# Even mixer of a hybrid trunk: S5 inputs projected first, S5 passes moved ahead, gate products put inside the heads, tables loaded from GpSimd's queue

## The chip, the cores and the metric

The kernel runs on one core of a Trainium2 chip. A core has five engines with a queue of instructions each: TensorE (PE, matmuls), VectorE (DVE), ScalarE (ACT), GpSimd (POOL) and SyncE (SP, which here only issues DMAs). Each engine works its queue in order; a semaphore makes it wait for another engine or for a DMA. The metric is the device time of one execution in microseconds (us), the median of several.

## The reference, cut to what matters

A trunk of two layers, each a half feed-forward step, a mixer and another half step, on 256 latent and 256 context tokens of width 1024. Layer 0 has the even mixer, which the change is about: attention over a latent (low rank) projection beside an S5 state-space stream.

```python
def even_mixer(h_ctx, h_lat, ...):
    cq, ckv, kr, s = split(h @ w_in, [384, 640, 672])       # widths 384, 256, 32, 512
    k_lat, v_lat = mla_keys_values(ckv, kr, kv_norm, w_ukv, cos, sin)
    q_lat = mla_queries(cq, q_norm, w_uq, cos, sin)          # rmsnorm, 8 heads of 64 + 32 rope
    o_lat = latent_attention(q_lat, k_lat, v_lat, k_ctx, v_ctx)
    s_lat_out, _ = s5_stream(s, ...)
    return concatenate([o_lat, s_lat_out]) @ w_out

def s5_stream(u, ...):                                       # 32 groups of 16 channels, 64 states
    for dr in range(2):                                      # forward and backward in time
        h = linear_scan(a, einsum('gpc,bngc->bngp', b_bar, u))
        y += real(einsum('gcp,bngp->bngc', c_mat, h))
    y = gelu(y + d_skip * u)
    return y * sigmoid(y @ w_glu + b_glu)
```

## The kernel before, in words

All matmuls of the dense layers (`mm3`, lines 154 to 163) split both operands into a high and a low part in fp32r and do three matmuls for each 128 rows of the inner dimension. `wload` brings a weight on SP's queue, ACT casts its high part (line 150), DVE subtracts to get the low part (line 151). There are four buffers for raw and four for split weights, six PSUM tiles `mm` and two `ps`. The Tile framework orders each engine's instructions when the program is built; the order of the code gives it what depends on what and what comes first among equals.

While the first feed-forward step runs, a background job (`s5_chunk`, eight chunks) makes the S5 tables in DRAM: `d_mb`, `d_g`, `d_v` and `d_e`. The even mixer then runs in this order. `norm_proj` normalises the stream and does the first three projections in one loop, the blocks of `EVEN` (7 and 8: the keys' latent; 4: the first third of the queries'). The other blocks follow: 5, 6 (queries' latent), 9 (the rope part of the keys), 0 to 3 (S5 input `u`, which goes to DRAM as `d_u` and comes back rearranged as `ut`). `low_norm` normalises the two latents: squares on ACT, a column of sums on PE (line 255), the inverse root in small DVE steps (lines 266 to 275), a spread over 128 rows on PE (line 284), a product on DVE (line 780) and a split (lines 166, 167). Then come the values, and four pairs of heads, each with keys and queries (rope: lines 887 to 892), and eight heads with scores (907 to 925), transposed probabilities (940 to 947) and values (959).

The S5 stream is cut into eight passes of four groups. A pass has two halves. `s5_states` loads `d_mb` and `d_e`, does 8 matmuls of 64 columns and a chain on DVE (lines 994 to 1009, with a scan at 1003) whose end is the tile `hh`. `s5_out` loads `d_g` and `d_v` (eight DMAs, line 1021), does 12 matmuls (1025 to 1027) and stores `d_y`. Pass 0 stands beside the queries of pair 1, passes 1 and 2 beside those of pairs 2 and 3, the others beside the scores of the heads, one by one; the last `s5_out` comes after the last score. Behind the heads `s5_act` loads `d_u` and `d_y` on SP's queue (36 DMAs), applies the skip and GELU (1045) and splits; `s5_glu` does four gate products of 12 matmuls, a sigmoid (1063) and a product (1064). Then comes the output projection. Tiles of the passes and of `s5_act` are slots of one pool `x` with ten buffers, which also holds the normalised input of the projections and `ut`.

Of the kernel before, what the change touches and what calls it, by code (L numbers as in the profile page):

```python
# [18 lines left out]
P = 128  # L19
# [8 lines left out]
H = 8  # L28
# [10 lines left out]
EVEN, ODD = (7, 8, 4), (12, 13, 14)  # L39
# [26 lines left out]
class Builder:  # L66
# [581 lines left out]
    def s5_chunk(self, q):  # L648
# [73 lines left out]
        nc.sync.dma_start(self.d_v[q], vt)  # L722
        yield
# [18 lines left out]
    def s5_prepare(self):  # L742
        dt = lambda nm, shape: [self.dram.tile(shape, F32, tag=f"{nm}{q}", name=f"{nm}{q}") for q in range(NPASS)]
        self.d_mb = dt("d_mb", [P, 8, P])
        self.d_g = dt("d_g", [P, 8, P])
        self.d_v = dt("d_v", [P, 240])
        self.d_e = dt("d_e", [P, 2, 8, 64])
        yield from self.s5_small()
        for q in range(NPASS):
            yield from self.s5_chunk(q)  # L750


    def even_mixer(self):
# [39 lines left out]
        ut = [self.slot("x", [P, 16, NCH]) for _ in range(2)]  # L793
        for i in range(4):
            u = self.slot("q", [P, L, NCH])
            nc.scalar.copy(u, self.proj("ev_in", i, xs, 0, T2).rearrange("p (c s) -> p s c", s=L))
            nc.scalar.dma_start(d_u[i * P : (i + 1) * P], u)
            if i == 0:
                st["ckv"] = low_norm(ckv, self.inv_kv, 3)
            elif i == 1:  # L800
                st["cq"] = low_norm(cq, self.inv_q, 0)
# [25 lines left out]
        def keys(p):  # L827
# [17 lines left out]
        vt = values_in()  # L845
        st["wk"] = self.wload(t["wuk"], D)
        qs, ks = [], []
        passes = iter(range(NPASS + 1))
# [3 lines left out]
        def s5_begin():  # L852
            i = next(passes, None)
            state.append(None if i is None or i == NPASS else self.s5_states(i, ut))
            return i

        def s5_end(i):
            if i:
                self.s5_out(i - 1, ut, d_y, state[i])

        for p in range(4):
            ks.append(keys(p))
            i = s5_begin() if p else None
            qs.append(queries(p))
            s5_end(i)
        os = []
        pend = None
        for h in range(H + 1):
            i = s5_begin()
            pr = self.scores(qs[h // 2][:, h % 2, :], ks[h // 2][:, h % 2, :]) if h < H else None  # L870
            s5_end(i)
            if h == H:
                fin = self.s5_act(d_u, d_y)
            if pend is not None:
                pts = self.probs_t(pend)
                if h % 2 == 1:
                    first = pts
                else:
                    os.append(self.values(h - 2, vt, (first, pts)))
            pend = pr  # L880
        os += self.s5_glu(*fin)
# [89 lines left out]
    def s5_states(self, q, ut):  # L971

        nc = self.nc
        mb = self.slot("x", [P, 8, P])
        nc.sync.dma_start(mb, self.d_mb[q])
        et = self.slot("x", [P, 2, 512])
        nc.sync.dma_start(et, self.d_e[q].rearrange("p e g c -> p e (g c)"))
# [11 lines left out]
        ta, tb = self.slot("x", [P, 2, 512]), self.slot("x", [P, 2, 512])  # L989
# [11 lines left out]
        nc.gpsimd.memset(rz[:, :, 0:1], 0.0)  # L1001
# [6 lines left out]
        nc.gpsimd.memset(hv[:, :, 0:1], 0.0)  # L1008
# [3 lines left out]
    def s5_out(self, q, ut, d_y, hv):  # L1012
        nc = self.nc
        u = ut[q // 4][:, (q % 4) * 4 : (q % 4) * 4 + 4, :]
# [566 lines left out]
```

## Time and profile before

| what | value |
|---|---|
| median of 3 runs | 1766.3 us (1765.08 to 1766.74) |
| the profiled execution, its span | 1764.04 us, 1762.0 us |
| PE busy | 1702.8 us, 97% of the span |
| DVE busy | 1267.6 us, 72% |
| ACT busy | 693.7 us, 39% |
| POOL busy | 13.2 us, 1% |
| chain that ended last | PE 89%, DVE 6%, DMA 2% |

The busy times of an engine are those of its own instructions; they overlap with those of the others. Starts are counted from the start of the span. The even mixer's body, from the last matmul of `norm_proj` to the output projection, is the stretch from 442.5 to 619.2 us. Where a row gives "x4" it is a run of four instructions; the fp32 matmuls of the scores and passes leave two records each in the trace. The pitch of an instruction is the distance from its start to the next one's, which leaves the overlap out.

### The profile page before, as it was taken

The numbers are of one execution on the slowest core, as the hardware profiler recorded it, in microseconds if no ns is written. First come the engines' busy times: TensorE is split into PE (matmuls) and PEld (weight loads), VectorE is DVE, ScalarE is ACT, GpSimd is POOL, SyncE is SP. The second block draws the span as 40 slices with busy tenths as digits, with TensorE's granted clock in tenths as the row PEclk, the third lists the DMA queues.
The fourth block names the chain that finished last, engine by engine and source line by source line (L and its number), as shares of the span: only waits on it lengthen the run. The fifth ranks groups of instructions, "written<-read, shape, count | busy, mean of one in ns | idle before, by whom it ended". The sixth has DMA issues, their size and how long they took to land.

```text
span 1762.0 us, 24867 instructions
## 1 busy us (share of the span) xinstructions
PE 1702.8 (97%) x9380; PEld 1443.5 (82%) x9380; DVE 1267.6 (72%) x2545; ACT 693.7 (39%) x1101; POOL 13.2 (1%) x47
## 2 busy tenths in 40 slices
PE   5999999999989999999999999999999999699998
PEld 3788878889878788778888888888888888499998
DVE  7999999987488668776676686555543576976675
ACT  4433333443445654222222233222222357554443
POOL 0000000000000000000000000000000000000000
PEclk9999999999998999999999999999999999899999
DMA  9566767662465453564554443555533225155552
GB/s 330 172 221 213 228 212 229 215 189 95 126 188 166 132 188 107 171 216 147 164 190 157 159 141 124 181 185 155 169 120 96 96 96 187 67 171 189 183 183 90
DMA packets 107480, 292.65 MB, mean 166 GB/s; under 512 B 21152, under 2 KB 35360, under 8 KB 107104
## 3 DMA queue, kind: packets, MB, share of 16 engines
q1 hardware_dynamic: 101504, 286.86, 50.6%
q10 hardware_dynamic: 5216, 2.62, 0.8%
q0 software_dynamic: 640, 1.57, 0.3%
q8 instruction: 74, 1.21, 0.3%
q14 instruction: 46, 0.38, 0.1%
HBM read 272.20 MB, written 18.28 MB: 165 GB/s over the span
## 4 chain that ended last, share of the span: by engine, by line
PE 89%; DVE 6%; DMA 2%; issue 1%; SPq 1%; ACT 1%; DVEq 0%; ACTq 0%
PE mm L160 25%; PE mm L162 25%; PE mm L161 25%; PE mm L157 7%; DVE w L151 1%; DMA h<-in_modw_dram 1%; PE mm L1207 1%; SPq L1040 1%; DMA x<-d_g 1%; PE mm L907 1%; DVE x L322 0%; DVE nt L315 0%; PE mm L191 0%; PE ps L690 0%; PE ps L1118 0%
## 5 line engine op out<-in xcount | busy, mean ns | idle before, releaser
L150 ACT CAST w<-raw 128x1024 fp32r<-128x1024 f32 (+2 forms) x324 | 328.8, 1019 | 530.6 <-PE mm L162 262.2
L161 PE MATMUL mm<-x,w 128*128 128x512 f32 (+1 forms) x1424 | 519.8, 365 | 0.0
L162 PE MATMUL mm<-x,w 128*128 128x512 f32 (+1 forms) x1424 | 519.2, 365 | 0.0
L160 PE MATMUL mm<-x,w 128*128 128x512 f32 (+1 forms) x1424 | 514.6, 367 | 3.5 <-ACT x L320 2.2
L151 DVE TENSOR_TENSOR w<-raw,w 128x1024 fp32r<-128x1024 f32 (+2 forms) x324 | 383.8, 1186 | 150.5 <-ACT w L150 149.3
L160 PEld LDWEIGHTS mm<-x,w 128*128 128x128 f32 x1424 | 267.4, 189 | 49.5 <-ACT x L320 2.5
L161 PEld LDWEIGHTS mm<-x,w 128*128 128x128 f32 x1424 | 268.6, 189 | 43.8 <-issue 2.0
L162 PEld LDWEIGHTS mm<-x,w 128*128 128x128 f32 x1424 | 268.5, 189 | 43.9 <-issue 1.2
L227 DVE CUSTOM_DVE_ANT_0 junk<-m,sc 128x1024 f32<-128x1024 f32 x224 | 273.0, 1219 | 1.8 <-DMA m<-in_modw_dram 0.4
L160 PE MATMUL mm<-h,w 128*128 128x512 f32 x456 | 178.3, 394 | 0.0
L162 PE MATMUL mm<-h,w 128*128 128x512 f32 x456 | 176.9, 390 | 0.0
L161 PE MATMUL mm<-h,w 128*128 128x512 f32 x456 | 176.7, 390 | 0.0
L435 DVE SCALAR_TENSOR_TENSOR res<-mm,mraw,res 128x256 f32<-128x256 f32 x192 | 86.0, 479 | 96.5 <-PE mm L162 87.2
L471 DVE TENSOR_TENSOR h<-h,mm 128x512 f32<-128x512 f32 x66 | 45.3, 686 | 108.1 <-PE mm L162 95.8
L470 ACT ACTIVATE h<-mm 128x512 f32<-128x512 f32 x66 | 39.5, 598 | 196.0 <-PE mm L162 185.2
L160 PEld LDWEIGHTS mm<-h,w 128*128 128x128 f32 x456 | 85.6, 188 | 18.9 <-issue 1.1
L162 PEld LDWEIGHTS mm<-h,w 128*128 128x128 f32 x456 | 85.6, 188 | 18.5 <-issue 0.6
L161 PEld LDWEIGHTS mm<-h,w 128*128 128x128 f32 x456 | 85.6, 188 | 18.4 <-issue 1.0
L160 PE MATMUL mm<-hy,w 128*128 128x258 f32 x352 | 99.2, 284 | 0.7 <-DVE g L499 0.7
L162 PE MATMUL mm<-hy,w 128*128 128x258 f32 x352 | 99.6, 283 | 0.0
L161 PE MATMUL mm<-hy,w 128*128 128x258 f32 x352 | 99.6, 283 | 0.0
L157 PE MATMUL mm<-x,w 128*128 128x256 f32 x384 | 66.3, 290 | 6.7 <-DVE x L322 6.2
(371 smaller groups left out, 2002.1 us busy)
## 6 DMA issues: line engine op xcount, KB each, us to landing
raw<-in_wgu_dram SPq DMA_DIRECT2D x176, 512.0 KB, 3.9
m<-in_modw_dram SPq DMA_DIRECT2D x130, 512.0 KB, 4.3
raw<-in_wd_dram SPq DMA_DIRECT2D x64, 512.0 KB, 3.6
raw<-in_wd_dram SPq DMA_DIRECT2D x32, 384.0 KB, 3.3
raw<-in_od_in_dram SPq DMA_DIRECT2D x20, 512.0 KB, 3.5
h<-in_modw_dram SPq DMA_DIRECT2D x12, 512.0 KB, 10.0
raw<-in_ev_in_dram SPq DMA_DIRECT2D x10, 512.0 KB, 3.5
d_mb<-mbt SPq DMA_DIRECT2D x16, 256.0 KB, 3.4
```

The costliest lines, as they stand in the source:

```text
L150: nc.scalar.copy(hi[:, :n], raw[:, :n])
L151: nc.vector.tensor_sub(lo[:, :n], raw[:, :n], hi[:, :n])
L157: mm = lambda *a, **k: self.keep(self.nc.tensor.matmul(*a, **k))
L160: mm(ps, lhsT=wh, rhs=xh, start=first and i == 0, stop=False)
L161: mm(ps, lhsT=wh, rhs=xl, start=False, stop=False)
L162: r = mm(ps, lhsT=wl, rhs=xh, start=False, stop=last and i == n - 1)
L227: nc.vector.tensor_tensor_reduce(self.junk, w, self.sc[:, v, :], 1.0, 0.0, ALU.mult, ALU.add, raw[:, dt, v : v + 1])
L435: self.nc.vector.scalar_tensor_tensor(r, ps[:, c0:c1], gate[:, i, VEC[h] : VEC[h] + 1], r, op0=ALU.mult, op1=ALU.add)
L470: nc.scalar.activation(s[:, 0, lo:hi], pg[:, lo:hi], AF.Silu)
L471: nc.vector.tensor_mul(s[:, 1, lo:hi], s[:, 0, lo:hi], pu[:, lo:hi])
L907: nc.tensor.matmul(ps, lhsT=q[0:96, c : c + P], rhs=k[0:96, :nk], start=True, stop=True)
L1040: nc.sync.dma_start(uy[g * 16 : (g + 1) * 16, 1, :].rearrange("p (s n) -> p s n", s=L), d_y[i * 8 + g].rearrange("s c n -> c s n"))
```

## The change

Seven things change, all in the even mixer but for one.

1. `EVEN` is (0, 1, 2): the S5 inputs are projected first, then block 3, and their way through DRAM to `ut` starts there. Blocks 7, 8, 4, 5, 6, 9 follow.
2. The passes start earlier: pass 0 beside block 4, pass 1 beside block 6, pass 2 beside the values, pass 3 beside pair 0, pass 4 beside pair 2, passes 5, 6, 7 beside the scores of heads 1, 2, 4. The last `s5_out` stands beside the score of head 5.
3. `s5_act` is called at head 5, and the first gate products inside heads 7 and 8; the order in which the output projection takes its operands is changed to fit.
4. `d_mb`, `d_e`, `d_g` and the last table are loaded on GpSimd's queue, not SP's.
5. The eight DMAs from `d_v` become one from `d_z`, a rearranged copy that `s5_chunk` makes with four GpSimd DMAs in each chunk.
6. The stores of `d_y` go from GpSimd's queue to ACT's; eight copies of `kr` into the keys are DVE copies of 32x512 and no longer GpSimd DMAs; 16 small memsets go from GpSimd to DVE.
7. Tables and work tiles of passes 0 and 1 are slots of the pool `q`.

```diff
-EVEN, ODD = (7, 8, 4), (12, 13, 14)
+EVEN, ODD = (0, 1, 2), (12, 13, 14)
...
         nc.sync.dma_start(self.d_v[q], vt)
+
+        dv = self.d_v[q]
+        for g in range(4):
+            nc.gpsimd.dma_start(
+                self.d_z[q][:, g, :].rearrange("(r c) m -> r c m", r=L),
+                bass.AP(dv.tensor, dv.offset + g * 32 * 240, [[16, L], [240, 16], [1, P]]),
+            )
...
-        ckv = low(pss[:2])
-        cq = low(pss[2:] + [self.proj("ev_in", i, xs, 0, T2) for i in (5, 6)])
-        st["kr"] = self.slot("kr", [P, T2])
-        self.rope(st["kr"], self.proj("ev_in", 9, xs, 0, T2), ropet)
...
-                nc.gpsimd.dma_start(k[64:96, h, :], st["kr"][64:96])
+                nc.vector.tensor_copy(k[64:96, h, :], st["kr"][64:96])
...
+        def with_pass(work):
+            i = len(state) - 1
+            state.append(self.s5_states(i, ut) if i < NPASS else None)
+            r = work()
             if i:
                 self.s5_out(i - 1, ut, d_y, state[i])
+            return r
...
+        ckv = low([project(7), project(8)])
+        cq = [with_pass(lambda: project(4)), project(5)]
+        st["ckv"] = low_norm(ckv, self.inv_kv, 3)
+        cq = low(cq + [with_pass(lambda: project(6))])
+        st["kr"] = self.slot("kr", [P, T2])
+        self.rope(st["kr"], project(9), ropet)
+        st["cq"] = low_norm(cq, self.inv_q, 0)
+        vt = with_pass(values_in)
+        st["wk"] = self.wload(t["wuk"], D)
+        with_pass(lambda: pair(0))
+        pair(1)
+        with_pass(lambda: pair(2))
+        score = lambda h: self.scores(qs[h // 2][:, h % 2, :], ks[h // 2][:, h % 2, :])
+        pend = score(0)
+        pair(3)
+        os, glu = [], None
+        for h in range(1, H + 1):
+            pr = None
+            if h < H:
+                pr = with_pass(lambda: score(h)) if h in (1, 2, 4, 5) else score(h)
+            if h == 5:
+                glu = self.s5_glu(*self.s5_act(d_u, d_y))
+            pts = self.probs_t(pend)
...
+            if h > 6:
+                os.append(next(glu))
             pend = pr
-        os += self.s5_glu(*fin)
+        os = os[:3] + [os[4]] + [os[3]] + os[5:] + list(glu)
...
-        mb = self.slot("x", [P, 8, P])
-        nc.sync.dma_start(mb, self.d_mb[q])
-        et = self.slot("x", [P, 2, 512])
-        nc.sync.dma_start(et, self.d_e[q].rearrange("p e g c -> p e (g c)"))
+        tag = "q" if q < 2 else "x"
+        mb = self.slot(tag, [P, 8, P])
+        nc.gpsimd.dma_start(mb, self.d_mb[q])
+        et = self.slot(tag, [P, 2, 512])
+        nc.gpsimd.dma_start(et, self.d_e[q].rearrange("p e g c -> p e (g c)"))
...
-        gm = self.slot("x", [P, 8, P])
-        nc.sync.dma_start(gm, self.d_g[q])
-        tz = self.slot("x", [P, 4, P])
-        dv = self.d_v[q].rearrange("(g c) m -> c g m", g=4)[0:16]
-        for r in range(L):
-            nc.sync.dma_start(tz[r * 16 : (r + 1) * 16], dv[:, :, r * 16 : r * 16 + P])
+        gm = self.slot(tag, [P, 8, P])
+        nc.gpsimd.dma_start(gm, self.d_g[q])
+        tz = self.slot(tag, [P, 4, P])
+        nc.gpsimd.dma_start(tz, self.d_z[q])
...
-        nc.gpsimd.dma_start(d_y[q * 4 : (q + 1) * 4].rearrange("g s c n -> (s c) g n"), ys)
+        nc.scalar.dma_start(d_y[q * 4 : (q + 1) * 4].rearrange("g s c n -> (s c) g n"), ys)
```

The built program of the changed kernel shows where things stand. In what follows `mm` and `ps` are PSUM tiles, `c` the split latents, `p` the latents and the probabilities, `x` and `hh` the tiles of passes. First PE around the norm of the queries' latent. Before, 46 rows (of the built order) lie between the column sums (line 255) and the spread of the inverse root (line 284); this is the start of that stretch:

```order
L284 MATMUL ps_4267<-ident,rs_y_4274 128x128 x4
L255 MATMUL ps_4357<-inv_q,p_4348 128x1 x4
L162 MATMUL mm_4422<-x_3880,w_4419 128x512
L160 MATMUL mm_4422<-x_3881,w_4419 128x512
L161 MATMUL mm_4422<-x_3881,w_4419 128x512
```

and this its end, inside the values:

```order
L821 MATMUL mm_4513<-w_4492,c_4312 128x512
L822 MATMUL mm_4513<-w_4492,c_4312 128x512
L284 MATMUL ps_4356<-ident,rs_y_4363 128x128 x4
L823 MATMUL mm_4513<-w_4492,c_4312 128x512
L821 MATMUL mm_4521<-w_4492,c_4308 128x512
```

After, the spread stands two rows behind the sums:

```order
L1038 MATMUL ps_4488<-hh_4300,q_4484 128x64
L255 MATMUL ps_4555<-inv_q,p_4546 128x1 x4
L162 MATMUL mm_4727<-c_4423,w_4695 128x512
L284 MATMUL ps_4554<-ident,rs_y_4561 128x128
L998 MATMUL ps_4610<-x_4162,x_4606 128x64 x4
L1000 MATMUL ps_4610<-x_4162,x_4606 128x64 x4
L284 MATMUL ps_4554<-ident,rs_y_4561 128x128 x3
L1036 MATMUL ps_4677<-x_4162,q_4675 128x64
L1037 MATMUL ps_4677<-hh_4441,q_4673 128x64
L1038 MATMUL ps_4677<-hh_4441,q_4673 128x64
```

What was covered by block 1, part of block 2 and half of the values has one matmul of the keys between; the states of the third pass (lines 998, 1000) and the outputs of the second (1036 to 1038) come next.

Second, ACT in the last heads. `ACT_TABLE_LOAD` loads a set of activation functions. Before, the heads end (lines 916 to 947) and then the GELUs (1045) and the sigmoids (1063) follow:

```order
L947 COPY c_5557<-mm_5564 128x4x128
L941 COPY c_5632<-mm_5633 128x512
L1029 COPY ys_5439<-ps_5426 128x256
L947 COPY c_5639<-mm_5640 128x4x128
L1045 ACT_TABLE_LOAD
L1045 ACTIVATE x_5572<-x_5572 128x512
L947 COPY c_5639<-mm_5646 128x4x128
L166 CAST x_5584<-x_5572 128x512
L166 CAST q_5665<-mm_5652 128x512
L1045 ACTIVATE x_5587<-x_5587 128x512
L166 CAST x_5599<-x_5587 128x512
L1045 ACTIVATE x_5602<-x_5602 128x512
```

After, GELU (line 1056) stands between the exponentials (927) of the heads; this is head 6:

```order
L927 ACTIVATE p_5380,sm_st_5381<-mm_5382,sm_st_5381 128x256 x2
L1056 ACT_TABLE_LOAD
L1056 ACTIVATE x_5428<-x_5428 128x512
L166 CAST q_5377<-mm_5364 128x512
L166 CAST x_5440<-x_5428 128x512
L927 ACT_TABLE_LOAD
L927 ACTIVATE p_5392,sm_st_5393<-mm_5394,sm_st_5393 128x512
L927 ACTIVATE p_5392,sm_st_5393<-mm_5396,sm_st_5393 128x512
L1040 COPY ys_5423<-ps_5410 128x256
L952 COPY c_5488<-mm_5489 128x512
L936 ACTIVATE p_5392<-p_5392,sm_st_5393 128x512 x2
L958 COPY c_5495<-mm_5496 128x4x128
```

Each of the four GELUs of the changed kernel has a table load ahead of it and another behind it: eight loads from the first GELU to the first sigmoid, where there were two.

Third, the loads of the tables. Before, they share SP's queue with the raw weights:

```order
L144 DMA raw_5766<-in_ev_out_dram 128x1024
L1017 DMA x_4740<-d_g_138 128x1024
L1021 DMA x_4742<-d_v_146 16x4x128 x8
L975 DMA x_4779<-d_mb_132 128x1024
L977 DMA x_4781<-d_e_156 128x1024
L144 DMA raw_5802<-in_ev_out_dram 128x1024
L144 DMA raw_5840<-in_ev_out_dram 128x1024
L144 DMA raw_5878<-in_ev_out_dram 128x1024
L1017 DMA x_4845<-d_g_139 128x1024
L1021 DMA x_4847<-d_v_147 16x4x128 x8
```

After, they are alone on GpSimd's queue, in the order in which the passes need them, but for the first two passes' `d_g` and `d_z`, which stand behind the `d_mb` and `d_e` of the third:

```order
L987 DMA q_4285<-d_mb_130 128x1024
L989 DMA q_4287<-d_e_162 128x1024
L987 DMA q_4426<-d_mb_131 128x1024
L989 DMA q_4428<-d_e_163 128x1024
L987 DMA x_4606<-d_mb_132 128x1024
L989 DMA x_4608<-d_e_164 128x1024
L1030 DMA q_4484<-d_g_138 128x1024
L1032 DMA q_4486<-d_z_154 128x512
L1030 DMA q_4673<-d_g_139 128x1024
L1032 DMA q_4675<-d_z_155 128x512
L987 DMA x_4698<-d_mb_133 128x1024
L989 DMA x_4700<-d_e_165 128x1024
```

## Rows read from the trace of the kernel before

**Rows 1.** PE by stretch: us, busy (instructions), granted clock, DMA share, GB/s.

```profile
523.00:530.00 7.00, 0.00 (x0) 0.78 0.68 199
530.00:545.00 15.00, 14.75 (x60) 0.53 0.62 197
```

**Rows 2.** PE's waits, 440 to 660 us: us in total, times, longest.

```profile
PE ps L1025 <- DMA x<-d_v: 7.4, 1, 7.4
PE mm L959 <- ACT c L947: 1.2, 1, 1.2
PE mm L162 <- DVE w L151: 0.6, 1, 0.6
PE mm L160 <- ACT x L166: 0.4, 1, 0.4
...
PE mm L160 <- ACT w L150: 0.4, 1, 0.4
```

**Rows 3.** Waits of SP's DMA queue, 440 to 620 us.

```profile
SPq L1017 <- DVE x L995: 22.2, 4, 6.6
```

**Rows 4.** The chain that ended last, at the wait: start, us, what.

```profile
523.17 4.92 DMA x<-d_g
```

**Rows 5.** Timeline of PE: start, us, line, tiles, run length.

```profile
519.15 1.06 PE L988 MATMUL ps<-x,x 128*128 128x64 f32 x8
520.05 2.80 PE L907 MATMUL mm<-q,q 96*128 96x256 f32 x8
...
599.42 0.39 PE L1026 MATMUL ps<-hh,x 128*128 128x64 f32 x2
599.64 0.39 PE L1027 MATMUL ps<-hh,x 128*128 128x64 f32 x2
...
601.20 1.04 PE L946 MATMUL mm<-ident,p 128*128 128x128 f32 x8
...
615.91 1.08 PE L160 MATMUL mm<-x,w 128*128 128x512 f32 x4
616.83 0.39 PE L161 MATMUL mm<-x,w 128*128 128x512 f32 x1
```

**Rows 6.** Timeline of DVE where passes and queries overlap.

```profile
504.05 0.69 DVE L151 TENSOR_TENSOR w<-raw,w 128x512 fp32r<-128x512 f32 x1
504.66 1.22 DVE L1003 TENSOR_TENSOR_SCAN x<-x,x 128x512 f32<-128x512 f32 x1
505.91 0.75 DVE L892 TENSOR_TENSOR q<-q,nt 32x256 f32<-32x256 f32 x2
506.68 0.69 DVE L1004 TENSOR_TENSOR x<-x,x 128x512 f32<-128x512 f32 x1
507.38 0.69 DVE L994 TENSOR_TENSOR x<-x,x 64x512 f32<-64x512 f32 x1
508.08 0.69 DVE L995 TENSOR_TENSOR x<-x,x 64x512 f32<-64x512 f32 x1
...
523.21 1.29 DVE L913 TENSOR_REDUCE sm_st<-mm 128x1 f32<-128x512 f32 x2
```

**Rows 7.** Timeline of DVE in the inverse root of the queries' latent.

```profile
478.82 0.60 DVE L273 SCALAR_TENSOR_TENSOR rs_a<-rs_y,rs_v 128x1 f32<-128x1 f32 x4
479.34 0.36 DVE L275 SCALAR_TENSOR_TENSOR rs_y<-rs_a,rs_y 128x1 f32<-128x1 f32 x4
```

**Rows 8.** Timeline of ACT: exponential, scaling, PSUM copies, table load, GELU.

```profile
526.80 0.68 ACT L916 ACTIVATE p<-mm,sm_st 128x512 f32<-128x512 f32 x1
...
530.61 1.33 ACT L925 ACTIVATE p<-p,sm_st 128x512 f32<-128x512 f32 x2 [2.36 <-DVE sm_st L919]
...
589.26 1.09 ACT L947 COPY c<-mm 128x512 f32<-128x512 f32 x2
...
602.45 1.28 ACT L1045 ACT_TABLE_LOAD   x1
603.75 0.63 ACT L1045 ACTIVATE x<-x 128x512 f32<-128x512 f32 x1
```

**Rows 9.** DMA issues of GpSimd's queue: size, median us to landing.

```profile
d_y<-ys POOLq DMA_DIRECT2D x8, 128.0 KB, 2.9
```

More of the change, by code (lines that the diff above doesn't have):

```diff
@@ L746, in s5_prepare @@
         self.d_v = dt("d_v", [P, 240])
+        self.d_z = dt("d_z", [P, 4, P])
         self.d_e = dt("d_e", [P, 2, 8, 64])
@@ L793, in even_mixer @@
         ut = [self.slot("x", [P, 16, NCH]) for _ in range(2)]
+        project = lambda i: self.proj("ev_in", i, xs, 0, T2)
         for i in range(4):
             u = self.slot("q", [P, L, NCH])
-            nc.scalar.copy(u, self.proj("ev_in", i, xs, 0, T2).rearrange("p (c s) -> p s c", s=L))
+            nc.scalar.copy(u, (pss[i] if i < 3 else project(i)).rearrange("p (c s) -> p s c", s=L))
             nc.scalar.dma_start(d_u[i * P : (i + 1) * P], u)
[L798 to L801, printed above, removed]
             if i % 2:
@@ L843, in queries @@
             return q
-        vt = values_in()
-        st["wk"] = self.wload(t["wuk"], D)
         qs, ks = [], []
-        passes = iter(range(NPASS + 1))
         state = [None]
[L852 to L857, printed above, removed]
+        def with_pass(work):
+            i = len(state) - 1
+            state.append(self.s5_states(i, ut) if i < NPASS else None)
+            r = work()
@@ L858, in s5_end, with pair @@
             if i:
                 self.s5_out(i - 1, ut, d_y, state[i])
-        for p in range(4):
+            return r
+        def pair(p):
             ks.append(keys(p))
-            i = s5_begin() if p else None
             qs.append(queries(p))
[L865 to L879, printed above, removed]
+        ckv = low([project(7), project(8)])
@@ new lines, in even_mixer @@
+        pend = score(0)
[8 more added lines that the diff above has]
+            pts = self.probs_t(pend)
+            if h % 2 == 1:
+                first = pts
+            else:
+                os.append(self.values(h - 2, vt, (first, pts)))
+            if h > 6:
+                os.append(next(glu))
@@ L988, in s5_states @@
                 nc.tensor.matmul(o.rearrange("p (t c) -> p t c", t=2), lhsT=mb[:, k, :], rhs=rev(u[:, g, :]), start=True, stop=True)
-        ta, tb = self.slot("x", [P, 2, 512]), self.slot("x", [P, 2, 512])
+        ta, tb = self.slot(tag, [P, 2, 512]), self.slot(tag, [P, 2, 512])
         hh = self.slot("hh", [P, 512])
@@ L1000, in s5_states @@
         rz = tb[:, 1].rearrange("p (g c) -> p g c", g=8)
-        nc.gpsimd.memset(rz[:, :, 0:1], 0.0)
+        nc.vector.memset(rz[:, :, 0:1], 0.0)
         nc.scalar.copy(rz[:, :, 1:NCH], self.s5["rho"][:, q * 8 : q * 8 + 8].unsqueeze(2).to_broadcast([P, 8, NCH - 1]))
@@ L1007, in s5_states @@
         xv, yv = (a.rearrange("p (g c) -> p g c", g=8) for a in (x, y))
-        nc.gpsimd.memset(hv[:, :, 0:1], 0.0)
+        nc.vector.memset(hv[:, :, 0:1], 0.0)
         nc.vector.tensor_add(hv[:, :, 1:NCH], xv[:, :, 0 : NCH - 1], yv[:, :, 0 : NCH - 1])
@@ L1013, in s5_out @@
         nc = self.nc
+        tag = "q" if q < 2 else "x"
         u = ut[q // 4][:, (q % 4) * 4 : (q % 4) * 4 + 4, :]
         rev = lambda a: a.rearrange("p (t c) -> p t c", t=2)[:, :, ::-1]
-        gm = self.slot("x", [P, 8, P])
-        nc.sync.dma_start(gm, self.d_g[q])
-        tz = self.slot("x", [P, 4, P])
-        dv = self.d_v[q].rearrange("(g c) m -> c g m", g=4)[0:16]
-        for r in range(L):
-            nc.sync.dma_start(tz[r * 16 : (r + 1) * 16], dv[:, :, r * 16 : r * 16 + P])
+        gm = self.slot(tag, [P, 8, P])
+        nc.gpsimd.dma_start(gm, self.d_g[q])
+        tz = self.slot(tag, [P, 4, P])
+        nc.gpsimd.dma_start(tz, self.d_z[q])
         py = self.ps()
```

4 lines of the change are left out of this document (1 added, 3 removed).

## The prediction

> **What bounds the kernel now.** The page's first part says PE: 97% of the span, and the chain that ended last is PE for 89%. PE has little idle time to give back, so I looked for where it loses time in the mixer's body, 442.5 to 619.2 us. The waits of PE [rows 2] show one large one, 7.4 us, in front of the first S5 output of pass 1, for the tile loaded from `d_v`. [...] Half speed there costs 14.75 x 0.47 = 6.9 us. The chain [rows 4] and SP's waits [rows 3] show why the load was late: `d_g` of that pass was issued at 523.17 only, since its slot of the pool `x` was still being read by DVE (L995), and the `d_v` loads queue behind it. So behind the DMA stands DVE, which had been working without a gap. The other waits of the body are 1.2 + 0.6 + 0.4 + 0.4 = 2.6 us [rows 2], all near its end. Together PE loses 7.4 + 6.9 + 2.6 = 16.9 us in the body. That is all that a new order can win: the matmuls are the same.
>
> **The change part by part.** *What goes.* The wait of pass 1's output for `d_v` goes as it stood (its load has moved to another queue, its slot comes from the pool `q`), and the slow stretch behind it: 14.3 us. The 2.6 us near the end go with the gate products, which no longer stand alone there. I count -16.9 us.
>
> *The queries' norm.* Before, 45 matmuls and small ones lie between the sums (L255) and the spread (L284); after, one. DVE's root needs three rounds of 0.6 + 0.36 us less overlap [rows 7], 0.9 each, and three single steps of about 0.15, so 3 us, and PE has 0.23 us of work meanwhile. A wait of some 3 us; it is the first part of what comes next, and not added to it.
>
> *The stretch from that norm to the second head's transposes.* Here the new order puts passes 2 to 5, all query pairs and three heads' scores. PE's work in it: 91 matmuls of 512 columns at 0.23 (four from 615.91 to 616.83) [rows 5], 20.9; four outputs of 12 at 0.22 (the 0.22 from 599.42 to 599.64), 10.8; five states at 1.8 (their second half runs from 519.15 to 520.05), 9.0; three scores at 2.7, 8.1; twelve transposes at 0.13, 1.6; sums and spreads 0.9: 51.3 us [rows 5]. DVE's work in it: a pass is a scan at 1.25 and eight operations at 0.70, 6.85, and two memsets of under 0.1: four passes 28.0. Rope is 24 operations at 0.41, 9.9 [rows 6]. Five weight subtractions, 3.3. Three heads' maxima at 0.64 each with the small ones, 7.5 [rows 6]. The root 3.0 [rows 7], three products and three splits at 0.67, 4.0. Six of the eight new DVE copies, 32x512: no row shows one. [...] I take 0.45, nearest to the row of the same 32 partitions, 2.7. Sum 58.4, and 2.3 us in which DVE waits for the states of pass 2 behind the spread: 60.7. PE works in order, and its last rows here (transposed probabilities of head 1) need DVE's last ones, so PE loses 60.7 - 51.3 = 9.4 us. Bounds: with copies at 0.2 and half of DVE's wait covered, 7; with copies at 0.7 and each of the two score releases late by an exponential, 13. The moved `kr` copies and memsets cost nothing elsewhere: DVE has room in the projections and after head 2.
>
> *Between head 2 and head 6* PE and DVE are level and a few waits for scaled probabilities remain: 2 us, from 0 to 4, by the 1.2 us wait of L959 for ACT, which I expect about twice [rows 2].
>
> *GELU inside the heads.* From head 6's first exponentials to the last copy of transposed probabilities ACT has, one behind the other: six table loads at 1.30 (602.45 to 603.75), 7.8; six exponentials at 0.66 and six of half the width at 0.46 (an estimate from the former), 6.8; six scalings at 0.62, 3.7; twelve PSUM copies at 0.48, 5.8 [rows 8]; five casts and three GELUs at 0.6, 4.7; a store's issue and a copy, 0.8. Sum 29.6 us. PE's work in the same stretch is one S5 output, two scores, four heads' transposes, one values (3.2) and nine matmuls of the first gate product: 2.7 + 5.4 + 6.4 + 3.2 + 2.1 = 19.8 [rows 5]. PE waits for exponentials and copies in turn, so it loses 9.8 us. Before, these heads had no table load between them. Bounds: 0, if ACT enters the stretch ten microseconds ahead of PE; 13, if GELU also waits for its `d_y` there, since exponentials queue behind a GELU.
>
> [...]
>
> *Moved at no cost.* SP's queue loses 88 issues and gains none, so raw weights come earlier; the cover was there already. The 32 copies to `d_z` stand behind the `d_v` store on GpSimd's queue, with the next chunk's memset behind them; a chunk lasts over 40 us, GpSimd is 1% busy, and what it delays is background work under the dense first feed-forward: 0, up to 2 if a chunk slips into the mixer. The `u` stores and the first `ut` loads go to ACT 25 us earlier in the code, ahead of the casts of weights 4, 5 and 6; PE has two blocks (10 us) in front of the first states. 0, up to 3. The `d_y` stores add eight issues to ACT, of which one is in the sum above.
>
> *Sum.* -16.9 + 9.4 + 2.0 + 9.8 = +4.3 us. Against the profiled execution's own 1764.04 that is 1768.3; that execution lies 2.3 us under the median of the runs, so the forecast for the median is 1770.6, say **1771 us**. Its own range, from the bounds of the two large terms, is 1769.9 to 1778. New waits of 3 us could also bring the lower clock back; half of the old price, 3.5 us, is inside that range.
>
> **The rivals.** *A: faster.* The place is the last heads: ACT is not the bound there. If PE reaches head 6 late, as the DVE stretch makes it, ACT may have copied and scaled ahead by then; the table loads vanish under PE's work and the 9.8 go to 0, with the DVE stretch at its lower bound 7: -16.9 + 7 + 1.5 = -8.4, 1758 us. It decides from the point where ACT has a lead of over 6 us at head 6. For it: ACT is busy 39% of the span. Against: exponentials need scores that PE has just made, so ACT can't run far ahead.
>
> *B: no change that can be measured.* Half of the ACT term hidden: +4.3 - 4.9, 1765.7 us. A measurement of this kernel tells about 0.2%, 3.5 us, from no change.
>
> *C: the wait moves to GpSimd's queue.* The loads of `d_g` and `d_z` still need slots that DVE releases, and now stand in order behind the next passes' loads. If pass 2's `d_z` (slot released at the end of its chain on DVE) lands after PE is there, PE has another wait like the old one, 7.4 us at most, with or without the lower clock: 1771 + 7.4 = 1778 us and up to 1785. For it: the mean wait for such a slot was 5.5 us, 22.2 in 4 [rows 3]. Against: PE itself is late at that point, waiting for the same DVE, and GpSimd's DMAs land in 2.9 us in the median [rows 9]. [...]
>
> **How the numbers follow.** The forecast (slower, 1769.9 to 1778) has 0.42, A 0.20, B 0.26, C 0.12. Slower by over 0.2% (above 1769.8): 0.42 + 0.12 = 0.54. Within: 0.26. Faster: 0.20. The range that should hold 8 in 10 goes from 1757, which leaves out about half of A, to 1780, which leaves out half of C. Signs on both sides hold much of the chance; the likeliest case's own range stands above.
>
> **What would show it.** In the changed kernel's profile: no wait for `d_v` or `d_z` of over 2 us (else C); a wait of about 3 us of L284 for DVE; DVE busy without a gap from there until head 1's scores, and PE under 90% busy in that stretch; six table loads between the exponentials of the last heads, ACT without a gap there and PE waiting for ACT some 10 us in all; a clock of 1.00 in the projections. The body should be 4 us longer than 176.7. If PE is dense in the last heads, the ACT term is wrong; if DVE shows gaps in the stretch of passes 2 to 5, the DVE term is; a lower clock over a long stretch would put the time above the range.

## The result, and the profile after

The changed kernel takes 1775.1 us (median of 4 runs, 1774.8 to 1776.1), the kernel before, run beside it, 1765.7 (1764.1 to 1766.7). The ratio is 1.0057, with a 95% interval of 1.0044 to 1.007: slower by 9.4 us. The forecast was 1771 and slower, with a range from 1757 to 1780. So the sign and the range held, and the loss is about twice the forecast. The profiled execution has a span of 1772.9 us, 10.9 more than before, and all of it is in the mixer's body: the first matmul of the output projection on the attention's operands starts at 630.03 us, where it started at 619.16 before.

The page's first part (busy us, share of the span, instructions):

```profile
PE 1713.2 (97%) x9380; PEld 1449.5 (82%) x9380; DVE 1272.1 (72%) x2569; ACT 701.3 (40%) x1107; POOL 37.2 (2%) x79
```

PE does the same matmuls and is busy 10.4 us longer; the share of 97% hides it. Most of it is what matmuls at the lower clock look like on that line (the granted clock reads 0.50 or 1.00 in 1752 of 1760 windows of 1 us before and in 1748 after): by these windows, what the clock lacks (busy time times what it is short of 1.00) grew from 6.9 to 12.3 us in the body, and by 3.5 us behind it, where the span did not get longer. PE's waits between 436 and 660 us (us in total, times, longest):

```profile
PE mm L951 <- DVE p L934: 3.3, 1, 3.3
PE ps L284 <- DVE rs_y L275: 2.7, 1, 2.7
PE mm L957 <- ACT p L936: 2.4, 1, 2.4
PE mm L957 <- ACT p L927: 0.9, 1, 0.9
...
```

The old wait of 7.4 us for `d_v` [rows 2] has no heir: no row names a table. In its place stand a wait for the queries' norm, one for a probability that DVE scales, and a handful for ACT, 13.0 us in all where there were 10.4. The windows by stretch show where the body's time went (after the stretch and its length: busy us and instructions of PE, PEld, DVE, ACT, POOL; then the granted clock, DMA share, GB/s):

```profile
442.50:493.60 51.10, 51.10 (x266) 43.51 (x266) 33.85 (x70) 20.85 (x34) 5.27 (x10) 1.00 0.71 206
493.60:516.00 22.40, 18.83 (x78) 17.36 (x78) 16.00 (x49) 4.51 (x8) 2.11 (x4) 0.54 0.34 104
516.00:545.00 29.00, 29.00 (x163) 24.64 (x162) 26.59 (x55) 14.53 (x36) 4.24 (x8) 1.00 0.50 155
545.00:564.00 19.00, 15.75 (x91) 12.49 (x91) 17.97 (x41) 12.10 (x32) 2.13 (x4) 0.91 0.60 203
564.00:587.00 23.00, 23.00 (x156) 17.03 (x155) 18.16 (x40) 14.25 (x35) 2.21 (x4) 1.00 0.43 116
587.00:620.00 33.00, 26.86 (x141) 17.03 (x140) 13.26 (x33) 32.02 (x61) 0.00 (x0) 0.95 0.18 44
```

Read each as idle time plus busy time times what the clock lacks. From 493.6 to 516: 3.6 idle and 18.83 x 0.46 = 8.7, so 12.3 us. From 545 to 564: 3.25 + 1.4 = 4.7. From 587 to 620: 6.1 + 1.3 = 7.4. The other stretches are dense at full clock. Sum 24.4 us, against 17.3 before (10.4 of waits and 6.9 of half clock). The slow stretch is no longer 15 us at pass 1's output [rows 1] but 20 at the queries' norm. PE's timeline there (start, us, line, tiles, run length; in brackets the wait ahead of it):

```profile
493.60 0.48 PE L162 MATMUL mm<-c,w 128*128 128x512 f32 x1
496.81 0.76 PE L284 MATMUL ps<-ident,rs_y 128*128 128x128 f32 x2 [2.72 <-DVE rs_y L275]
497.36 1.81 PE L998 MATMUL ps<-x,x 128*128 128x64 f32 x8
498.96 1.91 PE L1000 MATMUL ps<-x,x 128*128 128x64 f32 x8
```

The four matmuls of the states' second half (two records each) take 1.91 us at line 1000; before they took 1.06 [rows 5]. DVE, which follows PE there, shows the other side (its marked idle times from 493 to 545 of 0.6 us or more):

```profile
493.78 0.16 DVE L266 TENSOR_SCALAR rs_v<-ps 128x4 f32<-128x4 f32 x1 [0.60 <-PE ps L255]
500.91 0.69 DVE L1009 TENSOR_TENSOR x<-ps,x 128x512 f32<-128x512 f32 x1 [4.04 <-PE ps L1000]
513.19 0.69 DVE L1009 TENSOR_TENSOR x<-ps,x 128x512 f32<-128x512 f32 x1 [1.84 <-PE ps L1000]
543.37 0.17 DVE L930 RECIPROCAL sm_st<-sm_st 128x2 f32<-128x2 f32 x1 [0.68 <-ACT p L927]
```

And ACT in the last heads, where it is busy 32.0 of 33 us: each GELU between two table loads, two of the eight shown.

```profile
587.90 1.28 ACT L1056 ACT_TABLE_LOAD   x1
589.19 0.63 ACT L1056 ACTIVATE x<-x 128x512 f32<-128x512 f32 x1
...
590.83 1.28 ACT L927 ACT_TABLE_LOAD   x1
592.13 0.69 ACT L927 ACTIVATE p<-mm,sm_st 128x512 f32<-128x512 f32 x1
```

### The profile page after: what moved, and what is told of

Same layout as the page of the kernel before. It is cut to its first block, busy times and chain, and to the rows that moved or that the text cites. A ratio compares the mean times of both kernels' runs of the same rounds, so it can differ in the third digit from the quotient of the medians.

```text
span 1772.9 us, 24792 instructions
## 1 busy us (share of the span) xinstructions
PE 1713.2 (97%) x9380; PEld 1449.5 (82%) x9380; DVE 1272.1 (72%) x2569; ACT 701.3 (40%) x1107; POOL 37.2 (2%) x79
## 4 chain that ended last, share of the span: by engine, by line
PE 88%; DVE 7%; ACT 2%; issue 1%; DMA 1%; SPq 0%; DVEq 0%; ACTq 0%
PE mm L160 25%; PE mm L161 25%; PE mm L162 25%; PE mm L157 7%; DVE w L151 1%; PE mm L1216 1%; DMA h<-in_modw_dram 1%; DMA raw<-in_wgu_dram 1%; DVE x L322 0%; ACT p L927 0%; PE mm L970 0%; PE ps L284 0%; DVE nt L315 0%; PE ps L690 0%; PE ps L1127 0%
```

## The experiments

Three things can have cost the time: the norm that lost its cover, DVE's full queue behind it, and the table loads in the heads. Two theories on the first two: either the lower clock is the price by itself, or DVE sets when the stretch ends, and PE's waits and clock only fill the time until then. "Body" is the start of that output projection's matmul; a ratio is that to the kernel before, run beside it.

**The norm covered.**

```diff
-            rb = self.rstd([acc], inv)
+            r = self.rstd_stats([acc], inv)      # sums and root here,
+            ...                                  # spread (rstd_rows), product and split in low_rest
-        st["cq"] = low_norm(cq, self.inv_q, 0)
+        r = low_norm(cq, self.inv_q, 0, split=True)
         vt = with_pass(values_in)
+        st["cq"] = low_rest(cq, r, 0)
```

> The changed kernel with the spread of the queries' inverse root put, in the code, behind the third pass and the values; in the built order 8 state matmuls of the third pass and 12 output matmuls of the second then stand between the column sums and the spread, 4 to 5 us of work at full clock. Theory 1 (the price of the clock): the wait of 2.7 us for DVE goes, PE keeps its upper clock from 495 to 516, where the changed kernel ran about 20 us at half, and the time falls by 9 to 12 us against the changed kernel, to 1763 to 1766. Theory 2 (DVE is the bound there, whatever PE's clock): DVE had gaps of only 0.6 + 4.0 + 1.8 = 6.5 us from 493 to 543, so no more than that can be won, 3 to 6.5 us, to 1769 to 1772, and PE waits more in front of head 1's transposes than the 3.3 us of now.

Measured: 1770.5 us, ratio 1.0028 [1.0017, 1.0039], 4.7 us less than the changed kernel; body 624.55, 5.5 less. PE's waits there, and two windows of PE (busy, instructions, clock, DMA share, GB/s):

```profile
PE mm L956 <- DVE p L939: 2.4, 1, 2.4
PE mm L160 <- ACT c L166: 2.4, 1, 2.4
...
PE ps L284 <- DVE rs_y L275: 0.6, 1, 0.6
```

```profile
490.00:500.00 10.00, 9.81 (x80) 1.00 0.40 121
500.00:510.00 10.00, 7.23 (x36) 0.85 0.51 164
```

The wait for the norm falls to 0.6 us, the 20 us at half clock shrink to about 4, and yet only 5.5 us are won: a new wait of 2.4 us for the split of the same latent appears at once. DVE is now busy from 495 to 559 us with marked gaps of 0.7 us in all. That is the size that the second theory gave; its other sign missed, as the wait in front of head 1's transposes did not grow from 3.3 us but fell to 2.4. The way from the column sums (line 255) to those transposes is 59.8 us, where it was 67.4. Of the nine executions, the one with the highest mean clock (0.991) took 1767.9 us and the one with the lowest (0.984) 1776.1; the profile is one of them, of 1769.3 us.

**The gate products behind the heads.**

```diff
-            if h == 5:
+            if h == H:
                 glu = self.s5_glu(*self.s5_act(d_u, d_y))
...
-            if h > 6:
-                os.append(next(glu))
-        os = os[:3] + [os[4]] + [os[3]] + os[5:] + list(glu)
+        os += list(glu)
...
-            nc.scalar.activation(y, y, AF.Gelu_apprx_tanh)
+            self.keep(nc.scalar.activation(y, y, AF.Gelu_apprx_tanh))   # behind ACT's earlier instructions
```

> The changed kernel with the skip and GELU called at the last step of the heads and all four gate products behind the heads, each GELU held behind the activations written ahead of it: two table loads from the heads' end to the first sigmoid in place of eight. Theory 1 (ACT's table loads cost PE's time in the last heads): PE's waits for ACT from 590 to 618, about 5 us, and the half clock behind them, about 2, go, and some 2 to 3 us of waits for the gate's chain come back as in the kernel before: 4 to 5 us less, 1770 to 1771. Theory 2 (the loads lie beside other work, the waits come from the heads' own chain): within 2 us of the changed kernel, 1773 to 1777, or slower since the gate products no longer cover the last heads.

Measured: 1772.5 us, ratio 1.0041 [1.0026, 1.0056], 2.6 less than the changed kernel; body 625.48, 4.55 less. ACT has one load for the four GELUs (at 607.86), and from 590 to 610 PE's clock is 1.00:

```profile
PE mm L968 <- ACT c L950: 1.7, 1, 1.7
```

One wait of 1.7 us for the last probabilities is left there, and four of 0.4 to 0.5. So GELU inside the heads cost PE's time: 4.55 us by the body, which is the first theory's size, and 2.6 us by the median, which lies between the two theories, with an interval that overlaps with the changed kernel's. The edit takes the four GELUs, their casts and the gate products out of the heads together with six loads, so the share of the loads alone is not shown.

**Both.**

```diff
+ the edit of "The norm covered"
+ the edit of "The gate products behind the heads"
```

> Both edits in one. If the two costs are independent, the sum of the two differences. Theory 1: 13 to 17 us less than the changed kernel, 1758 to 1762, below the kernel before by 4 to 8. Theory 2 (DVE bound and loads hidden): 3 to 8 us less, 1767 to 1772, slower than the kernel before still.

Measured: 1764.1 us, ratio 0.999 [0.998, 0.9999], body 619.54, 10.5 less than the changed kernel and 0.4 more than before. By the body of one profile each the two costs add up (5.5 + 4.55 = 10.05 of 10.5); by the medians it is 4.7 + 2.6 = 7.3 of 11.0. Together they are all of the change's loss. What remains, the passes spread from the projections on, the tables' queue and the copies on DVE, is worth 0.1% against the kernel before, at the edge of what can be told.

**The tables alone, in the kernel before.**

```diff
-        nc.sync.dma_start(mb, self.d_mb[q])
+        nc.gpsimd.dma_start(mb, self.d_mb[q])      # d_e, d_g too; d_z for d_v, made in s5_chunk
```

> The kernel before with one part of the change alone: the four tables on GpSimd's queue, the last one from the rearranged copy. The order of passes, heads and gate products stays. Theory 1 (the 7.4 us wait was for a slot that DVE held, so the queue doesn't matter): PE's longest wait for the tables of a pass stays at 4 to 8 us, time within 2 us of the kernel before, 1764 to 1768. Theory 2 (it was SP's queue with its eight small loads behind one another): the wait falls under 2 us, the half clock behind it goes, and the time falls by 8 to 14 us, to 1752 to 1758. Theory 3 (GpSimd's queue is the slower one, with memsets and the copies of kr behind waiting loads): slower by 3 us or more.

Measured: 1774.9 us, ratio 1.0054 [1.0037, 1.007], slower by 8.7 us. Its waits name two places:

```profile
PE ps L1031 <- DMA x<-d_z: 2.9, 2, 2.1
PE mm L948 <- DVE p L931: 2.9, 2, 1.9
PE mm L160 <- ACT c L166: 2.7, 1, 2.7
```

The first two are the old place: there is still a wait for the table and for DVE, 5.8 us where it was 7.4, with some 13 us at half clock (537 to 550). So the queue alone doesn't take it away. The third is new, and the chain of waits says how it came (start, us, what):

```profile
481.79 7.79 DMA d_u<-q
...
490.01 2.62 DMA x<-d_u
492.65 0.63 ACT c L166
...
493.32 0.79 PE mm L160
```

With the tables on a queue of their own their loads start earlier, and from 480 to 485 us the DMA engines are 0.96 busy, where they were 0.53. The store of `d_u` issued at 481.8 needs 7.8 us, where the same store needed 2.4 before; ACT, whose queue issues the loads behind it, stands still for 8.2 us, and the cast of the queries' latent behind them comes late. The third theory has the sign, but not the reason: PE's rows name no memset and no copy of `kr`, but the DMA engines were 0.96 busy. That this made the store late is read from the rows; no run tests it alone. The order of the two kernels also differs in some places that the edit doesn't name, so the 8.7 us are not split further.

**The kr copies on ACT**, on top of both.

```diff
-                nc.vector.tensor_copy(k[64:96, h, :], st["kr"][64:96])
+                nc.scalar.copy(k[64:96, h, :], st["kr"][64:96])
```

> The kernel with both edits (norm covered, gates last; 1764.1 us) and the eight copies of kr into the keys on ACT in place of DVE. Six of them lie in the stretch from the norm to head 1's transposes, where DVE had gaps of 0.7 us in 64; at 0.42 us each they are 2.5 us of DVE's work there. Theory 2 (DVE sets the end of that stretch): the time falls by 2 to 3 us, to 1761 to 1762, most of it from PE's waits for split latents and scaled probabilities (2.4 us each). Theory 1 (DVE has room and the waits come from chains through ACT): no gain, or slower by up to 2 us, since ACT's copies stand ahead of others.

Measured: 1762.8 us, ratio 0.9986 [0.9977, 0.9995], 1.3 less than without, though the two intervals overlap. The body ends 1.4 us earlier, about half of DVE's 2.5: DVE now shows gaps of 0.4 to 1.6 us for ropes that wait for ACT. It is the first of these kernels whose interval lies clearly under the kernel before.

**The passes one place later, with the copies on DVE and on ACT.**

```diff
-        with_pass(lambda: pair(0))
-        pair(1)
-        with_pass(lambda: pair(2))
+        pair(0)
+        with_pass(lambda: pair(1))
+        pair(2)
...
-                pr = with_pass(lambda: score(h)) if h in (1, 2, 4, 5) else score(h)
+                pr = with_pass(lambda: score(h)) if h in (1, 2, 3, 4, 6) else score(h)
```

> The kernel with both edits, and the passes shifted by one place from the fourth on: none beside pair 0, the fourth beside pair 1, then heads 1, 2, 3, 4, the last output beside head 6. One pass (7 us of DVE, 4.4 us of PE) leaves the stretch up to head 1's transposes and goes to the heads, where DVE is busy 27 of 40 us. Theory 2 (DVE is the bound): PE's time falls by the difference, 2 to 4 us, to 1760 to 1762, and the 2.4 us wait in front of head 1's transposes falls under 1. Theory 1 (waits are chains of single operations): within 1 us of 1764, as the chains stay. A third way: the passes now end two heads later, and GELU with its last store waits at the end, 2 to 3 us more.

> Both of these in one. Theory 2: once DVE is no longer the bound of the stretch by the shifted pass, the copies give less than their 2.5 us: 1759 to 1761. Theory 1: 1764 or more.

Measured: 1769.5 us (1.0017 [1.0008, 1.0026]) and 1766.0 us (0.9999 [0.9991, 1.0008]), 5.4 and 3.2 slower than with the passes where they were. The third way has the sign; the first two theories miss. Up to head 1's transposes the first of the two is level with the kernel that it is built on (59.6 and 59.9 us from the column sums); its body ends 4.9 us later, all of it behind them. With the copies on DVE:

```profile
PE mm L960 <- ACT p L939: 3.4, 1, 3.4
PE mm L960 <- DVE nt L905: 3.1, 2, 2.9
```

```profile
540.00:550.00 10.00, 8.98 (x40) 0.63 0.18 59
550.00:560.00 10.00, 10.00 (x44) 0.69 0.56 193
```

PE waits 2.9 us in the middle of head 0's transposes (at 541), and then loses 6.4 us to the clock up to 560 (8.98 x 0.37 + 10 x 0.31). The 3.4 us stand in the last heads (at 604), with 3 us of clock behind them: on ACT a table load and the first GELU (from 602.04) come ahead of the scaling that PE waits for, which is not the end that the third way named. Less work on the busiest engine did not make the stretch shorter: DVE's busy time in it fell by 4.7 us (56.7 to 52.0), and its idle time grew by as much, as the first theory has it. That PE has too little work of its own beside the heads' chains is a guess that no run tests. A sum over a stretch holds only where DVE has no gap.

**The tables back on SP's queue, in the changed kernel.**

```diff
-        nc.gpsimd.dma_start(mb, self.d_mb[q])
+        nc.sync.dma_start(mb, self.d_mb[q])        # d_e, d_g, d_z too
```

> The changed kernel with the four tables back on SP's queue (the rearranged copy kept, so four loads a pass). Theory A (in the new order the queue doesn't matter, since PE waits for DVE and not for tables): within 2 us of the changed kernel, 1773 to 1777, no wait of PE for a table over 1 us. Theory B (GpSimd's queue is what makes the changed kernel slow, as it made the kernel before slower by 8.7 us): faster by 4 us or more. Theory C (the queue is where the old 7.4 us were won, loads that wait for a slot hold up raw weights on SP's queue): slower by 3 to 10 us, with PE waiting for raw weights' splits.

Measured: 1773.8 us, ratio 1.0049 [1.0036, 1.0061], 1.3 less than the changed kernel, with intervals that overlap. PE waits for no table, the wait for the norm is 2.7 us as before the edit, and the clock from 500 to 510 is 0.50. So in the new order the queue is of no account that can be measured.

**The norm uncovered, in the kernel before.**

```diff
-            self.proj("ev_in", i, xs, 0, T2)
+            self.proj("ev_in", i, xs, 0, T2, i == 2)     # block 2's matmuls kept behind the spread
```

> The kernel before with the cover of the queries' norm taken away: the spread of its inverse root stands right behind the column sums on PE, ahead of blocks 2 and 3. DVE has gaps there, so what PE loses is not hidden by DVE. This measures the clock's price by itself. The wait should be 3 to 5 us (the root's 2.9 us, and the products and splits of the other latent between). Theory 1 (a wait of that length in a dense stretch brings the lower clock for 10 to 20 us): PE reaches the values 8 to 15 us later than in the kernel before, and the whole takes 6 to 15 us more. Theory 2 (the lower clock lasts some 3 us only, as after the 2.4 us waits of the last kernels): 4 to 7 us later there, and no more than that in the whole.

Measured: 1773.6 us, ratio 1.0044 [1.003, 1.0058]. The wait came out longer than expected, since a product of the other latent and a weight's subtraction share DVE with the root:

```profile
477.11 2.04 PE L284 MATMUL ps<-ident,rs_y 128*128 128x128 f32 x8 [5.96 <-DVE rs_y L275]
```

```profile
477.00:480.00 3.00, 2.90 (x11) 0.50 0.35 34
480.00:483.00 3.00, 3.00 (x14) 0.91 0.00 0
```

PE starts the values at 490.61 and not at 481.21, 9.4 us later: 6.0 of wait, 1.7 of lower clock (2.9 x 0.5 + 3.0 x 0.09), and 1.7 of rows that now stand ahead of the values, the spread among them. The lower clock lasted 3.4 us behind the wait, not 10 to 20, although the wait was twice that of the changed kernel. The whole lost 8.6 us, but not for this reason alone, as the wait in front of the heads also took another form (6.6 us for DVE at line 940).

**The softmax meant to go ahead of the passes on DVE, and the keys as cover.**

```diff
...
+            with self.tc.high_priority(offset=SOON):
                 nc.vector.reciprocal(st[:, 3, :], st[:, 2, :])          # the scalings too
```

> The kernel with the norm covered, gates last and the kr copies on ACT (1762.8 us), and the four small steps and the scaling of each softmax on DVE put ahead of the passes' operations by priority. The wait in front of head 1's transposes (2.5 us, then some 3 us at the lower clock) came from a scaling that stood behind three operations of a pass on DVE. If such queueing is the cause: the wait falls under 1 us, and the time by 2 to 4 us, to 1759 to 1761. If DVE's total work sets it: within 1 us of 1762.8.

```diff
-        with_pass(lambda: pair(0))
-        pair(1)
+        ks.append(keys(0))
+        ks.append(keys(1))                                   # kept in this order
+        with_pass(lambda: qs.append(queries(0)))
+        qs.append(queries(1))
```

> The kernel with the norm covered, gates last and the kr copies on ACT, and the keys of pairs 0 and 1 (12 matmuls, 2.8 us) held behind the spread of the queries' root, as cover for the split of the queries' latent, where PE waited 2.4 us for ACT's cast. If that wait is a chain to be covered: it falls under 0.5 us, the 3 us at the lower clock behind it go, 3 to 4 us less, 1759 to 1760. If DVE sets the end of the stretch whatever PE does: the 2.4 us come back as a wait for a pass's chain or a rope, within 1 us of 1762.8 or slower by the clock that a longer wait costs.

Measured: 1762.8 us (0.9984 [0.9975, 0.9993]) and 1767.1 us (1.0012 [1.0003, 1.002]). The first tests nothing of the softmax: PE and DVE run the same instructions in the same order as in the kernel that it is built on (the kr copies on ACT), and the scaling still stands behind the same three operations of a pass. It is that program run again, and by this chance it bears on the question. Its window at the queries' first matmuls, and that of the kernel that it is built on:

```profile
500.00:510.00 10.00, 9.34 (x34) 0.53 0.38 128
```

```profile
500.00:510.00 10.00, 7.60 (x37) 0.83 0.46 146
```

In the one PE runs at half clock from 500.5 to 510.7 and doesn't wait for the split, in the other it is at half clock for 3.4 us only and waits 2.4 us. Here are the column sums and head 1's transposes, first of the one, then of the other:

```profile
494.10 1.00 PE L255 MATMUL ps<-inv_q,p 128*128 128x1 f32 x8
554.59 0.63 PE L957 MATMUL mm<-ident,p 128*128 128x128 f32 x4 [2.54 <-ACT x L1020]
```

```profile
493.14 1.00 PE L255 MATMUL ps<-inv_q,p 128*128 128x1 f32 x8
553.47 0.63 PE L954 MATMUL mm<-ident,p 128*128 128x128 f32 x4 [2.54 <-ACT x L1017]
```

The way between them takes 60.49 and 60.33 us: with one program, 7 us more at half clock cost 0.2. In the second kernel the wait for the split went as expected, and came back in front of head 1's transposes, larger:

```profile
557.28 1.09 PE L956 MATMUL mm<-ident,p 128*128 128x128 f32 x4 [4.30 <-DVE p L939]
```

Here the way takes 64.7 us, 4.4 more, with the same DVE work: DVE's marked idle times from 495 us to the transposes are 6.5 us where they were 3.9, most of it for ACT; PE had run at half clock from 496.4 to 510 (0.50 in each window from 498 to 510). So the first pair says that PE's own loss is hidden where DVE has work to do, and the second kernel that a new order on PE moves the end all the same when DVE comes to wait by it.

**The last wait filled**, on top of the norm covered, gates last and copies on ACT.

```diff
         po = self.pm()
+        self.fill(po, 8 if h0 == H - 2 else 0)     # 8 matmuls of ident by ident, overwritten
```

> The kernel with the norm covered, gates last and the kr copies on ACT (1762.8 us), and eight matmuls of 128 columns whose result is overwritten, on PE in front of the last values, where PE waited 1.66 us for ACT's copy of the transposed probabilities and then ran 3.4 us at the lower clock. They take about 0.21 us each, 1.7 us, so they fill the wait and delay nothing. This is the clock's price with no order changed. Theory 1 (the wait itself brings the clock down, and a busy PE keeps it up): the clock reads 1.00 from 600 to 610, where it read 0.83, and PE ends the mixer 1.7 us earlier: 1761. Theory 2 (the clock falls there for another reason, or PE waits for the same chain a little later): no change of the clock, 1762.8 or up to 1.7 us slower.

Measured: 1762.3 us, ratio 0.9982 [0.9973, 0.9991], 0.5 less than the kernel without, which is within the runs' scatter. The rows show more, here the filled kernel's values and window, then those of the kernel without:

```profile
599.78 1.95 PE L945 MATMUL mm<-ident 128*128 128x128 f32 x16
601.66 3.43 PE L978 MATMUL mm<-c,v 128*64 128x256 f32 x24
```

```profile
600.00:610.00 10.00, 9.59 (x59) 1.00 0.00 0
```

```profile
601.43 4.49 PE L973 MATMUL mm<-c,v 128*64 128x256 f32 x22 [1.66 <-ACT c L955]
```

```profile
600.00:610.00 10.00, 8.15 (x37) 0.83 0.00 0
```

The clock stays at 1.00, and 24 matmuls of the values take 3.43 us where 22 took 4.49; the body ends 0.8 us earlier, half of the 1.7 expected. That looks like the first theory, but another run stands against it. The kernel with the gate products behind the heads has the same matmuls there, with no fill and the same wait:

```profile
610.30 2.92 PE L968 MATMUL mm<-c,v 128*64 128x256 f32 x22 [1.66 <-ACT c L950]
```

```profile
608.00:618.00 10.00, 7.95 (x43) 1.00 0.00 0
```

Its clock did not fall, and the 22 matmuls took 2.92 us. Of the five profiles that have this wait of 1.66 us without a fill, four show the lower clock behind it, at a price of 1.6 us (4.49 - 2.92), and one does not. So such a wait can have a second price; that the fill took it away in the one profile with a fill is not shown.

## Why the prediction was right in sign and short by half

*What goes, -16.9.* Right. The wait for `d_v` [rows 2], the slow stretch behind it (14.75 us busy at a clock of 0.53 [rows 1]) and the small waits near the end have no rows after. The reason given, slots that DVE held and not the queue, is borne out: with the new queue alone the place still waits, and with the old queue in the new order nothing does. (Of the small waits, the one of 0.6 us lies at 620.45, behind the body.)

*The queries' norm, a wait of 3 us.* Right, 2.72. It was "not added", as the first part of DVE's stretch.

*The stretch to head 1's transposes, +9.4.* This is the step that failed. DVE's work was sized well: the transposes start at 560.13, 66.35 us after DVE's first step of the norm; take off its marked idle times behind that step, 7.9 us (the last three rows above and three of 0.3 to 0.5 behind them), and 58.5 are left, where the forecast had 58.4, the copies among them at 0.42 us (0.45 taken). No run shows a copy at the 0.2 of the lower bound: in the changed kernel all eight took 0.42. What was short is "2.3 us in which DVE waits for the states of pass 2": it waited 4.0 us for them and 1.8 for those of the next pass, since PE made both at half clock. So the lower clock, which the forecast left at 0 in the sum ("half of the old price, 3.5 us, is inside that range"), came in through DVE's waits, 3.6 us over the forecast there and 5.6 in the stretch with the later gaps. PE's own loss by the windows is 12.3 + 4.7 = 17.0 against 9.4 forecast. The covered norm made the way from the sums to the transposes 7.6 us shorter, by about as much as DVE's marked waits fell (with the 0.6 in front of the norm, from 8.5 to 1.0), and 5.5 of it reached the body. By the forecast's own sign a lower clock over a long stretch would put the time above the range; it was low for 20 us and the time stayed inside.

*Between head 2 and head 6, +2.0.* Wrong, 0: PE is dense at full clock from 564 to 587.

*GELU in the heads, +9.8.* The mechanism was right, the size too large. From the first exponential of head 6 to the last copy ACT takes 30.1 us (29.6 forecast), but PE has more work in that time:

```profile
586.90:617.00 30.10, 23.95 (x129) 0.96 0.20 48
```

At full clock that is 23.95 x 0.96 = 23.0 us, where the forecast had 19.8, so PE loses 7.1 us and not 9.8. Moving GELU out gave 4.55 back, as waits of 2.9 us, the one of 1.7 among them, return without the gate products. Each of the eight table loads takes 1.28 us, and the next activation starts 0.01 to 0.02 us behind its end at seven of them; the eighth, a sigmoid, waits for PE. So the 7.8 us taken for six loads hold.

*Moved at no cost.* Right in the changed order, but the reason was incomplete: the same queue in the old order cost time, by the rows through the DMA engines (0.96 busy from 480 to 485 us), a resource that the forecast didn't weigh.

*The rivals.* A fell: ACT was the bound in the last heads. B fell with the sign: a quarter of the ACT term was hidden, not half. C fell: no wait for `d_z`, and the tables back on SP's queue gave 1.3 us. From 490 to 535 us the loads on GpSimd's queue landed in 4.2 us (`d_mb`), 5.8 (`d_e`) and 2.9 (`d_z`) in the changed kernel, in 5.1, 5.9 and 3.5 with both edits in, and in 4.5, 5.5 and 3.4 with the copies on ACT on top of both (medians of two loads each), and PE waited for none of them.

*The ledger.* Forecast +4.3 on the profiled execution, measured +10.9. The stretch is 7.6 over, the heads between 2.0 and the last heads 2.4 under: 3.2 of the 6.6 us. The other 3.4 lie in time in which the rows have PE busy, and no run places them. That the range held is in part luck: two terms that were too high made up for much of the one that was too low, and the lower end of the likeliest case's own range, 1769.9, does not come out of the bounds that it names (-16.9 + 7 + 2 + 0 is -7.9 us).

What stays open is when PE's clock falls. After the 2.72 us wait it stayed low for some 19 us (497 to 515.6), and as long in the two other kernels with the norm uncovered in the new order; after one of 5.96 for 3.4. With the keys as cover it fell at 496.4, behind a wait of 0.83, and stayed low until about 510, while in the kernel with the norm covered, with nearly the same matmuls there, it held. And it differs between executions of one program: with the copies on ACT it held behind a wait of 1.14 us at the norm's spread, and in the run again of that program it fell there, behind 0.66. The runs show what it costs once it has fallen, not which of these waits brings it down.

## What to carry to other kernels

A step that moves ahead loses what stood between its halves: look in the built order at what covers each small chain of one engine, and keep that cover when blocks are reordered. Where PE waits for an engine without gaps, count that engine's work and also its waits for PE; here neither PE's clock nor a better cover won more than those. A transfer that starts earlier on a new queue can meet a store that someone else waits for: with the tables' queue alone changed the DMA engines were 0.96 busy where they had been 0.53, and the store of `d_u` took 7.8 us and not 2.4; that the one made the other is read from the rows.

## What the runs showed of the hardware that was not expected

Short waits can have a second price: one of 1.66 us in front of the last values was followed by some 3 us at half clock in four profiles (0.83 in the window from 600 to 610 us with the `kr` copies on ACT), 1.6 us lost, and in a fifth, with the same matmuls and the same wait, the clock stayed at 1.00. One program, run again, spent 10 us and not 3.4 at half clock behind the norm (0.53 and 0.83 from 500 to 510 us), and the way to head 1's transposes took only 0.2 us longer, as DVE set its end. A store of 256 KB that landed in 2.4 us took 7.8 with the DMA engines 0.96 busy from 480 to 485 us and 0.63 from 485 to 490. And the four matmuls of 64 columns of a half of the states have a pitch of 0.9 us at a clock of 1.00 and 1.6 to 1.7 at 0.50, where one matmul of 128x512 has 0.23 and 0.43: the passes are about as sensitive to the clock as a dense product.
